# Four weight splits queued behind two transposed parts, and half of the merged sum transposed later

## The chip, the cores and the metric

The kernel runs on one core of one Trainium2 chip. The metric is device time of one execution in microseconds (us), lower is better; times are medians of repeated runs. The core's engines work side by side, each through its own queue in order: TensorE (PE; its weight loads are listed as PEld), VectorE (DVE), ScalarE (ACT), GpSimd (POOL), and SyncE (SP), which here only issues DMA transfers. An instruction starts when it is at the head of its queue and the semaphores it waits for have come.

## The reference

Two blocks in a row on 256 tokens of width 1024. The first normalises the tokens, projects them with `w_in`, runs dilated attention, a gated convolution and an attention to 256 memory rows, adds the three branches under gates, multiplies the sum with `w_out` onto the residual, and ends in a mixture of 32 experts, two per token. The second is a token mixer with scans and a feed-forward layer. What the change touches:

```python
kv  = rmsnorm(mem, g_mem) @ w_mem_kv      # memory: 256 x 1024 times 1024 x 1024
...
mg  = sum over branches of gate_b * (branch_b @ w_proj_b)   # 256 x 1024
x   = x + mg @ w_out                      # then the router, then the experts
```

## The kernel before, in words

**Products in two parts.** Every large product is made from operands cut in two: `hi`, a rounded copy, and `lo`, the remainder. `split` (L192) does this for 128 rows of a weight tile: ACT writes `hi` (L197), then POOL (L200) or DVE (L202), in turns, subtracts to give `lo`. `split_T` (L347) does it for activations that TensorE has transposed into PSUM: ACT writes the high part (L351), DVE the low part (L352) from the same PSUM bank. Two readers of one bank are kept apart, so the ACT copy of the next 128 columns waits for the DVE step of the ones before. `gemm_tm` (L227) then issues, for each of eight slices k and each of two token halves t, three products of 512 columns (L225): high part by `hi`, high part by `lo`, low part by `hi`. The split weights live in `hl`, five buffers for each part, so the splits run up to five slices ahead of the products.

**Generators.** After each slice `gemm_tm` calls `tick`, which advances work waiting in `self.side` by one `yield`.

**Order.** The code gives the order of the program. A planner of the framework (`schedule_with_timeline_sim`, L2102) then fixes each engine's queue by its own model of time: among the instructions that are ready in the model, it issues the one that stands earlier in the program. `issue_after(ins)` forces the instructions in its block behind `ins` on the same engine. The expert part up to its overflow test is planned in one piece with block 1.

**The start (L636 to L651).** The memory rows come in two halves of 512 columns, and the first two weight tiles of `w_mem_kv` (`w0`, four slices) beside them. `norm_T` (L365) transposes the memory (tile `pT`, four 128-column pieces in each of two tiles) and splits it into `hh` and `hl`; the scale is the gain `g_mem`, from `cols`. Then the product with `w_mem_kv`, columns 0 to 511 (keys), then 512 to 1023 (values).

**The merged sum (L717 to L762).** `mg` is held in two tiles, `mg[0]` for columns 0 to 511 and `mg[1]` for 512 to 1023. Its last contribution is added on DVE (`mt` L733, `mg` L735), for the second half right at the end of the last projection. L738 to L744 transpose both halves, four PSUM tiles `pmg` of two column pieces each, and split them into `mgh` and `mgl`. Then `eb.close()` gives back the space of `mg` and others, `open_first` opens five rings in it for early expert weights, and `w_out` is multiplied in two column halves, each over eight slices: slices 0 to 3 need `mg[0]`, slices 4 to 7 need `mg[1]`. The tag `acc` has four PSUM banks, shared by `pmg` and the two accumulators of each product. During the second column half the router's logits are begun (`first_half`).

Of the kernel before, what the change touches and what calls it, by code (L numbers as in the profile page):

```python
# [9 lines left out]
F32 = mybir.dt.float32  # L10
# [3 lines left out]
AF = mybir.ActivationFunctionType  # L14
# [35 lines left out]
def blocks(t):  # L50
    return [t[:, k, :] for k in range(t.shape[1])]


class Pools:


    def __init__(self, first, tags, second):
        self.of = lambda tag: first if tag in tags else second
# [5 lines left out]
class Builder:  # L64
# [21 lines left out]
    def __init__(self, tc, A, dbg):  # L86
        self.tc, self.nc, self.A, self.dbg = tc, tc.nc, A, dbg
        self.side, self.side2 = deque(), deque()
        self.started = False
        self.mem_first = self.lg = self.er = None  # L90
        self.first = []
        self.early = []
        self.mark = {}
        self.early_first = []
        self.ep = ExitStack()
        self.nt = 0
        self.pe = 0.0
        self.spent = 0.0
        self.es = ExitStack()
        self.nlo, self.lo, self.sp = 0, 2, 1024  # L100
# [77 lines left out]
    def wload(self, src, r0, n, c0, N, pairs=False):  # L178
# [10 lines left out]
        self.nc.sync.dma_start(out=t, in_=src[r0 * 128:(r0 + n) * 128, c0:c0 + N].rearrange("(k p) n -> p k n", p=128))  # L189
        return t  # L190

    def split(self, w, n, N):  # L192

        nc = self.nc
        hi = self.hl.tile([128, n, N], F32R, tag="hi", name="hi")
        lo = self.hl.tile([128, n, N], F32R, tag="lo", name="lo")
        nc.scalar.activation(out=hi, in_=w, func=AF.Copy)  # L197
        self.nlo += 1
        if self.nlo <= 0 or self.nlo % self.lo:
            nc.gpsimd.tensor_tensor(out=lo, in0=w, in1=hi, op=OP.subtract)  # L200
        else:
            nc.vector.tensor_tensor(out=lo, in0=w, in1=hi, op=OP.subtract)  # L202
        return hi, lo
# [143 lines left out]
    def split_T(self, ps, hi, lo, scale=None, imm=None):  # L347

        nc = self.nc
        s = scale if scale is not None else (1.0 if imm is None else imm)  # L350
        nc.scalar.activation(out=hi, in_=ps, func=AF.Copy, scale=s)  # L351
        nc.vector.scalar_tensor_tensor(out=lo, in0=ps, scalar=s, in1=hi, op0=OP.mult, op1=OP.subtract)  # L352

    def row_rstd(self, x):
# [10 lines left out]
    def norm_T(self, x, g, name, pool, normed=True):  # L365

        nc = self.nc
        hi = pool.tile([128, 8, 256], F32R, tag=name + "h", name=name + "h")
        lo = pool.tile([128, 8, 256], F32R, tag=name + "l", name=name + "l")
        xn = [x[:, t] for t in range(2)]  # L370
        if normed:
            r, xn = self.row_rstd(x)
            for t in range(2):
                nc.vector.tensor_scalar(out=xn[t], in0=x[:, t], scalar1=r[:, t:t + 1], scalar2=None, op0=OP.mult)
        for k in range(0, 8, 4):
            p = self.ps2.tile([128, 4, 256], F32, tag="ps2", name="pT")
            for j in range(4):
                for t in range(2):
                    nc.tensor.transpose(p[:, j, t * 128:(t + 1) * 128],
                                        xn[t][:, (k + j) * 128:(k + j + 1) * 128], self.ident)  # L380
            for j in range(4):
                self.split_T(p[:, j, :], hi[:, k + j, :], lo[:, k + j, :], scale=g[:, k + j:k + j + 1])
        return blocks(hi), blocks(lo)


# [218 lines left out]
    def block1(self):  # L604
        nc, A, tc = self.nc, self.A, self.tc
        es = ExitStack()
        ed = ExitStack()
        eb = ExitStack()
# [5 lines left out]
        def T(tag, name, shape, dt=F32, bufs=1):  # L614
            return (pa if tag in LATE else pb if tag in MID else self.pd).tile([128] + shape, dt, tag=tag, name=name, bufs=bufs)
# [30 lines left out]
        self.vm = T("a5", "vm", [2, 512])  # L646
        scaled = lambda dst: (lambda t, p: nc.scalar.activation(out=dst[:, t], in_=p, func=AF.Copy, scale=rm[0][:, t:t + 1]))
        self.early = w0
        self.gemm_tm(w_kv, 8, 0, 512, mT, scaled(self.km))
        self.load_x()  # L650
        self.gemm_tm(w_kv, 8, 512, 512, mT, scaled(self.vm))  # L651
# [65 lines left out]
        mg = [T(f"a{1 + i}", "mg", [2, 512]) for i in range(2)]  # L717
        for oi, (br, wn, nk) in enumerate([(2, "w_proj_mem", 4), (1, "w_proj_conv", 6), (0, "w_proj_attn", 2)]):
            bT = {0: (self.oah, self.oal), 1: (self.zh, self.zl), 2: (self.omh, self.oml)}[br]
            bT = [blocks(t) for t in bT]  # L720
            for half in range(2):
                G = T("G", "G", [2, 512], bufs=2)
                self.gemm_tm(w_in, 8, 5120 + br * 1024 + half * 512, 512, hT, lambda t, p: nc.scalar.activation(
                    out=G[:, t], in_=p, func=AF.Tanh, scale=0.5), tick=2)
# [10 lines left out]
                        nc.vector.tensor_tensor(out=d, in0=d, in1=m, op=OP.add)  # L735
                self.gemm_tm(A[wn][0], nk, half * 512, 512, bT, ev)
        mgh, mgl = T("hh", "mgh", [8, 256], F32R), T("hl", "mgl", [8, 256], F32R)
        for b in range(0, 8, 2):  # L738
            p = self.acc.tile([128, 2, 256], F32, tag="acc", name="pmg")
            for j in range(2):  # L740
                for t in range(2):
                    o = 128 * ((b + j) % 4)
                    nc.tensor.transpose(p[:, j, 128 * t:128 * t + 128], mg[b // 4][:, t, o:o + 128], self.ident)
            self.split_T(p, mgh[:, b:b + 2], mgl[:, b:b + 2], imm=0.5)  # L744
        lg = self.logits(self.acc, "acc", [T(f"a{6 + i}", "x1T", [4, 256]) for i in range(2)], lambda: T("mt", "junk", [512], bufs=2))

        def first_half():
            yield
            yield
            next(lg)  # L750

        self.drain()
        self.finish2()
        eb.close()
        self.open_first(self.nearly)
        for half in range(2):
            hs = slice(half * 512, half * 512 + 512)
            self.gemm_tm(A["w_out"][0], 8, half * 512, 512, (blocks(mgh), blocks(mgl)), lambda t, p: nc.vector.tensor_tensor(
                out=self.x[:, t, hs], in0=p, in1=self.x[:, t, hs], op=OP.add), late=self.late0 * half)
            if half == 0:  # L760
                self.side.append(first_half())
        self.drain()  # L762
        deque(lg, maxlen=0)
# [1342 lines left out]
```

## Time and profile before

| | us |
|---|---|
| median of 3 runs (lowest to highest) | 1489.14 (1488.11 to 1493.19) |
| profiled execution | 1496.53 |
| its span, first to last instruction | 1494.8 |
| PE busy in the span | 1374.6 |
| DVE / ACT / POOL busy | 839.4 / 632.1 / 571.4 |
| mean granted TensorE clock | 0.968 |

Matmuls overlap, so a duration listed for one is longer than its share of the time; the distance from one start to the next is the measure. A row of the timeline gives start, duration, engine, line, operation, output<-inputs and a count; rows of equal neighbours are merged. The square bracket is idle time of the engine before the row and what ended it. In the rows `hh`, `hl` are the parts of the transposed memory, `mgh`, `mgl` those of the merged sum.

### The profile page before, as it was taken

The numbers are of one execution on the slowest core, as the hardware profiler recorded it, in microseconds if no ns is written. First come the engines' busy times: TensorE is split into PE (matmuls) and PEld (weight loads), VectorE is DVE, ScalarE is ACT, GpSimd is POOL, SyncE is SP. The second block draws the span as 40 slices with busy tenths as digits, with TensorE's granted clock in tenths as the row PEclk, the third lists the DMA queues.
The fourth block names the chain that finished last, engine by engine and source line by source line (L and its number), as shares of the span: only waits on it lengthen the run. The fifth ranks groups of instructions, "written<-read, shape, count | busy, mean of one in ns | idle before, by whom it ended". The sixth has DMA issues, their size and how long they took to land. (4 is left out here: it accounts for less than half of the span.)

```text
span 1494.8 us, 25833 instructions
## 1 busy us (share of the span) xinstructions
PE 1374.6 (92%) x10187; PEld 1091.2 (73%) x10188; DVE 839.4 (56%) x1570; ACT 632.1 (42%) x1308; POOL 571.4 (38%) x438
## 2 busy tenths in 40 slices
PE   7999999999988898998898979998989799799997
PEld 6778877876655664765565649896889687699985
DVE  6684574444324646533465537888669965833334
ACT  6675434543313213120322225556747434455543
POOL 3433225441100012130002214478965634567764
PEclk9999999999999999999999999999999999899998
DMA  8758659976999999999989882521334214455551
GB/s 290 243 180 307 250 222 346 354 265 221 401 389 409 406 397 405 396 414 379 394 355 412 314 309 93 170 87 55 113 100 127 85 58 141 135 191 183 172 203 49
DMA packets 135307, 374.37 MB, mean 250 GB/s; under 512 B 12472, under 2 KB 26639, under 8 KB 123919
## 3 DMA queue, kind: packets, MB, share of 16 engines
q1 hardware_dynamic: 135183, 372.69, 67.6%
q8 instruction: 81, 1.33, 0.4%
q14 instruction: 43, 0.35, 0.1%
HBM read 371.61 MB, written 1.06 MB: 249 GB/s over the span
## 5 line engine op out<-in xcount | busy, mean ns | idle before, releaser
L200 POOL TENSOR_TENSOR lo<-w,hi 128x512 fp32r<-128x512 f32 x262 | 363.0, 1392 | 377.1 <-ACT hi L197 329.2
L197 ACT ACTIVATE hi<-w 128x512 fp32r<-128x512 f32 x436 | 270.2, 630 | 264.6 <-PE acc L225 243.5
L202 DVE TENSOR_TENSOR lo<-w,hi 128x512 fp32r<-128x512 f32 x174 | 156.5, 900 | 204.9 <-ACT hi L197 204.4
L225 PE MATMUL acc<-xh,lo 128*128 128x256 f32 x576 | 165.3, 289 | 3.4 <-DVE lo L202 3.4
L225 PE MATMUL acc<-xl,hi 128*128 128x256 f32 x576 | 166.6, 290 | 0.0
L225 PE MATMUL acc<-xh,hi 128*128 128x256 f32 x576 | 166.1, 290 | 0.0
L796 PE MATMUL gu<-w,xg 128*32 128x256 f32 x2048 | 132.6, 383 | 0.0
L225 PEld LDWEIGHTS acc<-xh,lo 128*128 128x128 f32 x576 | 112.5, 196 | 4.0 <-DVE lo L202 3.6
L225 PEld LDWEIGHTS acc<-xl,hi 128*128 128x128 f32 x576 | 112.9, 196 | 0.5 <-issue 0.2
L225 PEld LDWEIGHTS acc<-xh,hi 128*128 128x128 f32 x576 | 113.1, 197 | 0.2
L796 PEld LDWEIGHTS gu<-w,xg 128*32 128x32 f32 x2048 | 65.8, 110 | 50.9 <-issue 8.9
L225 PE MATMUL acc<-cT,w 128*128 128x256 f32 x416 | 99.2, 391 | 2.1 <-DMA w<-in_w_in_dram 2.1
L1423 POOL TENSOR_TENSOR U<-U,Z 128x512 f32<-128x512 f32 x32 | 41.4, 1296 | 150.0 <-DVE Z L1422 148.1
L225 PEld LDWEIGHTS acc<-cT,w 128*128 128x128 f32 x416 | 79.1, 195 | 22.3 <-issue 8.9
L1411 POOL TENSOR_TENSOR U<-U,Z 128x512 f32<-128x512 f32 x8 | 13.8, 1729 | 197.6 <-ACT y L827 99.0
L225 PE MATMUL acc<-lo,hh 128*128 128x512 f32 (+1 forms) x224 | 87.8, 394 | 0.0
L225 PE MATMUL acc<-hi,hl 128*128 128x512 f32 (+1 forms) x224 | 86.0, 393 | 1.2 <-DVE hl L352 1.2
L225 PE MATMUL acc<-hi,hh 128*128 128x512 f32 (+1 forms) x224 | 81.6, 398 | 5.5 <-ACT hh L351 5.5
L1304 DVE SCALAR_TENSOR_TENSOR cva<-acc,cwg,cva 128x248 f32<-128x248 f32 (+3 forms) x160 | 72.0, 473 | 19.7 <-ACT cva L1298 18.0
L825 DVE COPY y<-yq 32x256 f32<-32x256 f32 x64 | 27.0, 422 | 89.7 <-ACT y L827 89.3
L820 PE MATMUL yq<-w,hT 128*32 128x256 f32 x1024 | 71.3, 419 | 5.0 <-ACT hT L814 5.0
L1403 ACT ACTIVATE V<-U 128x512 f32<-128x512 f32 x40 | 25.7, 642 | 97.4 <-POOL U L1423 80.6
(539 smaller groups left out, 2908.2 us busy)
## 6 DMA issues: line engine op xcount, KB each, us to landing
w<-in_w_in_dram SPq DMA_DIRECT2D x71, 1024.0 KB
w<-in_w_gate_dram SPq DMA_DIRECT2D x64, 1024.0 KB
w<-in_w_up_dram SPq DMA_DIRECT2D x64, 1024.0 KB
w<-in_w_down_dram SPq DMA_DIRECT2D x64, 1024.0 KB
w<-in_w_ada_dram SPq DMA_DIRECT2D x24, 1024.0 KB
w<-in_w_out_dram SPq DMA_DIRECT2D x12, 1024.0 KB
w<-in_w_ffn_gate_dram SPq DMA_DIRECT2D x11, 1024.0 KB
w<-in_w_ffn_up_dram SPq DMA_DIRECT2D x11, 1024.0 KB
```

Of the source, the lines that this page charges most:

```text
L197: nc.scalar.activation(out=hi, in_=w, func=AF.Copy)
L200: nc.gpsimd.tensor_tensor(out=lo, in0=w, in1=hi, op=OP.subtract)
L202: nc.vector.tensor_tensor(out=lo, in0=w, in1=hi, op=OP.subtract)
L225: return self.nc.tensor.matmul(out, lhsT=lhsT, rhs=rhs, start=start, stop=stop, skip_group_check=True)
L796: last = nc.tensor.matmul(gu[32 * j:32 * j + 32, :], lhsT=xg[:, k, s0:s0 + 32], rhs=w[k // 4][:, k % 4, 256 * (j % 2):256 * (j % 2) + 256] ...
L820: nc.tensor.matmul(yq[32 * q:32 * q + 32, :], lhsT=hT[:, b, 32 * half:32 * half + 32], rhs=wd[kb // 2][:, kb % 2, 256 * q:256 * q + 256], ...
L825: nc.vector.tensor_copy(o, i)
L1304: nc.vector.scalar_tensor_tensor(out=av[:, :, d], in0=pv[:, :, s], scalar=wc(k), in1=av[:, :, d], op0=OP.mult, op1=OP.add)
L1403: nc.scalar.activation(out=cut(bt["V"], b), in_=view(bt["U"], b), func=AF.Copy)
L1411: nc.gpsimd.tensor_tensor(out=view(U, b), in0=view(U, b), in1=cut(Z, b), op=OP.add)
L1423: nc.gpsimd.tensor_tensor(out=view(U, b), in0=view(U, b), in1=cut(Z, b), op=OP.add)
```

## The change

`held` puts the next four ACT copies of `split` behind the instruction stored in `self.hold`. That is the second `split_T` of the memory (its columns 128 to 255), and the four copies are those of the first four weight slices. The transposes and splits of `mg[1]` become `merged(1)`, called from `self.side` at the third tick of the first `w_out` half, that is after its third slice in program order. `eb.close()` and `open_first` move behind the first half of `w_out`, since `mg[1]` is still needed.

```diff
+    def held(self):
+        n, after = self.hold
+        self.hold = n - 1, after
+        return self.tc.issue_after(after.ins) if n > 0 else ExitStack()
...
-        nc.scalar.activation(out=hi, in_=w, func=AF.Copy)
+        with self.held():
+            nc.scalar.activation(out=hi, in_=w, func=AF.Copy)
...
-        nc.scalar.activation(out=hi, in_=ps, func=AF.Copy, scale=s)
+        self.mark["parts"] = nc.scalar.activation(out=hi, in_=ps, func=AF.Copy, scale=s)
...
+                if k + j == 1:
+                    self.first_parts = self.mark["parts"]
...
+        self.hold = 4, self.first_parts
         self.gemm_tm(w_kv, 8, 0, 512, mT, scaled(self.km))
...
-        for b in range(0, 8, 2):
-            p = self.acc.tile([128, 2, 256], F32, tag="acc", name="pmg")
+        def merged(half):
+            for b in (4 * half, 4 * half + 2):
+                p = self.acc.tile([128, 2, 256], F32, tag="acc", name="pmg")
...
+        def merged_late():
+            yield
+            yield
+            merged(1)
+
+        merged(0)
...
-        eb.close()
-        self.open_first(self.nearly)
+        self.side.append(merged_late())
         for half in range(2):
...
             if half == 0:
+                eb.close()
+                self.open_first(self.nearly)
                 self.side.append(first_half())
```

## Rows read from the trace of the kernel before

**Rows 1.** The page's first part: busy us, share, instructions.
```profile
PE 1374.6 (92%) x10187; PEld 1091.2 (73%) x10188; DVE 839.4 (56%) x1570; ACT 632.1 (42%) x1308; POOL 571.4 (38%) x438
```
**Rows 2.** Windows: stretch, length, busy per engine, PEclk, DMA share, GB/s.
```profile
50.00:323.00 273.00, 273.00 (x1584) 215.64 (x1582) 159.83 (x280) 141.74 (x263) 105.51 (x75) 1.00 0.75 270
323.03:329.49 6.46, 4.55 (x17) 3.51 (x17) 3.49 (x6) 0.84 (x3) 1.14 (x1) 0.74 0.90 319
327.00:328.00 1.00, 1.00 (x4) 0.81 (x3) 0.00 (x0) 0.00 (x0) 0.00 (x0) 0.50 0.92 348
360.00:370.00 10.00, 9.38 (x112) 6.56 (x114) 6.62 (x39) 1.70 (x3) 0.00 (x0) 1.00 0.19 71
```
**Rows 3.** Timeline, all engines, around the merged sum's transposes.
```profile
321.99 1.04 PE L743 MATMUL pmg<-cst,mg 128*128 128x128 f32 x8
322.38 1.27 DVE L733 SCALAR_TENSOR_TENSOR mt<-G,acc 128x512 f32<-128x512 f32 x2
322.73 1.07 ACT L351 ACTIVATE mgh<-pmg 128x512 fp32r<-128x512 f32 x2
322.90 1.27 POOL L200 TENSOR_TENSOR lo<-w,hi 128x512 fp32r<-128x512 f32 x1 [0.99 <-ACT hi L197]
323.57 1.15 DVE L735 TENSOR_TENSOR mg<-mg,mt 128x512 f32<-128x512 f32 x1
324.64 0.68 DVE L352 SCALAR_TENSOR_TENSOR mgl<-pmg,mgh 128x512 fp32r<-128x512 f32 x1
324.78 0.44 PE L743 MATMUL pmg<-cst,mg 128*128 128x128 f32 x2 [1.75 <-DVE mg L735]
325.38 0.50 PE L225 MATMUL acc<-hi,mgh 128*128 128x512 f32 x1 [0.16 <-DVE mgl L352]
326.41 0.63 PE L225 MATMUL acc<-hi,mgh 128*128 128x512 f32 x1
326.83 0.63 PE L225 MATMUL acc<-lo,mgh 128*128 128x512 f32 x1
328.54 1.19 PE L743 MATMUL pmg<-cst,mg 128*128 128x128 f32 x6
329.49 0.48 PE L225 MATMUL acc<-hi,mgh 128*128 128x512 f32 x1
```
**Rows 4.** Timeline, all engines, the first product with the memory's weights.
```profile
7.74 0.19 DVE L343 COPY cols<-pcol 128x34 f32<-128x34 f32 x1 [1.88 <-PE pcol L342]
8.88 1.15 ACT L197 ACTIVATE hi<-w 128x512 fp32r<-128x512 f32 x2 [6.63 <-DMA w<-in_w_mem_kv_dram]
9.94 0.46 ACT L351 ACTIVATE hh<-pT,cols 128x256 fp32r<-128x256 f32 x1
10.45 1.22 PE L225 MATMUL acc<-hi,hh 128*128 128x512 f32 x2 [2.74 <-ACT hh L351]
11.33 0.47 DVE L352 SCALAR_TENSOR_TENSOR hl<-pT,cols,hh 128x256 fp32r<-128x256 f32 x1
11.84 0.47 ACT L351 ACTIVATE hh<-pT,cols 128x256 fp32r<-128x256 f32 x1 [0.41 <-DVE hl L352]
12.21 1.05 ACT L360 ACTIVATE xn<-mem 128x1024 f32<-128x1024 f32 x1
13.17 1.91 PE L379 MATMUL pT<-cst,mem 128*128 128x128 f32 x8
15.53 0.40 PE L225 MATMUL acc<-hi,hh 128*128 128x512 f32 x1
15.76 0.39 PE L225 MATMUL acc<-lo,hh 128*128 128x512 f32 x1
18.18 0.50 PE L225 MATMUL acc<-hi,hh 128*128 128x512 f32 x1 [0.20 <-ACT hh L351]
19.64 0.74 PE L225 MATMUL acc<-hi,hl 128*128 128x512 f32 x2 [0.27 <-DVE hl L352]
```
**Rows 5.** Waits of PE from 360 to 880 us: total, times, longest.
```profile
PE tph L812 <- DVE hh L809: 22.8, 19, 1.8
```

More of the change, by code (lines that the diff above doesn't have):

```diff
@@ L97, in __init__ @@
         self.pe = 0.0
+        self.hold = 0, None
         self.spent = 0.0
@@ L737, in block1 @@
         mgh, mgl = T("hh", "mgh", [8, 256], F32R), T("hl", "mgl", [8, 256], F32R)
-        for b in range(0, 8, 2):
-            p = self.acc.tile([128, 2, 256], F32, tag="acc", name="pmg")
[L740 to L744, printed above, removed]
+        def merged(half):
+            for b in (4 * half, 4 * half + 2):
+                p = self.acc.tile([128, 2, 256], F32, tag="acc", name="pmg")
+                for j in range(2):
+                    for t in range(2):
+                        o = 128 * ((b + j) % 4)
+                        nc.tensor.transpose(p[:, j, 128 * t:128 * t + 128], mg[half][:, t, o:o + 128], self.ident)
+                self.split_T(p, mgh[:, b:b + 2], mgl[:, b:b + 2], imm=0.5)
+        def merged_late():
[3 more added lines that the diff above has]
+        merged(0)
         lg = self.logits(self.acc, "acc", [T(f"a{6 + i}", "x1T", [4, 256]) for i in range(2)], lambda: T("mt", "junk", [512], bufs=2))
```

## The prediction

> **What bounds the kernel now.** I read the busy shares first, then the windows, then the timeline at the two places that the change touches. PE is busy 92% of the span [rows 1]. The windows say that before the experts this is close to a hard bound: PE is busy for all of the 273 us from 50 to 323 at a granted clock of 1.00 [rows 2]. So a gap of PE removed there moves everything after it, unless a later wait takes it back. At the merged sum there is such a gap: 6.46 us in which PE is busy 4.55, at a mean clock of 0.74, with 0.50 for the whole microsecond from 327 [rows 2]. 0.50 is 1.2 GHz, 1.00 is 2.4 GHz. The expert stretch from 366 to 860 us has PE busy 445.83 of 494.00 us and DMA at a share of 0.97 [rows 2]. Both restart from the first expert: between 360 and 370 us the DMA share is 0.19, as the rings are full and wait for PE to use weights. An earlier PE therefore starts the transfers earlier too, and I pass the gain through this stretch in full.
>
> **The second edit, at 323 us.** Before, eight transposes of `mg[0]` start at 321.99 and are over at 323.03. PE's next instruction is a transpose of `mg[1]`, which waits for DVE's last addition and starts at 324.78: an idle of 1.75 us. The first product comes at 325.38, since its accumulator takes the PSUM bank of the first `pmg`, which DVE's `mgl` has to release [rows 3]. The clock then falls: products start 0.42 us apart at 326.41 and 326.83, where 0.23 is the distance at full clock (15.53 to 15.76) [rows 3, 4]. Six more transposes follow at 328.54, and from 329.49 on the products run in a row. So 6.46 us hold eight products and eight transposes. At full clock these are 8 x 0.23 + 8 x 0.13 (1.04 over eight) = 2.9 us. At most 3.6 us can be won: about 1.9 of idle, the rest the half clock.
>
> After the change the first three slices of `w_out` (18 products) stand ahead of the `mg[1]` transposes. The two accumulators are now allocated right after two `pmg` and not four, so by the turn of the four banks they take those of the last projection, free when `mt` ends at 323.65 (322.38 + 1.27), the first half of that pair at about 323.0. The first product then waits for `mgh` alone: half of the pair that starts at 322.73, so 323.3 [rows 3]. The weights of these slices were split ahead; the last subtraction, on POOL, ends at 324.17. Until the low part exists PE has eight products that need only the high part (two slices, two token halves, `hi` and `lo`): 1.8 us, to 325.2. The low part ends at 325.32 (324.64 + 0.68) [rows 3]. New idle: 0.3 before the first product and 0.2 before the low part, 0.5 in all. Two waits of 0.20 and 0.27, 1.5 us apart, stand at 18.18 and 19.64 [rows 4], and the clock did not fall after them, so I keep it at full. The term is 3.6 - 0.5 = 3.1 us.
>
> What moves with it: eight transposes, two ACT copies, two DVE parts. They are late next: the transposes start after 18 products, 323.3 + 0.2 + 4.1 = 327.6, and end near 328.6; the first low part is there 0.5 + 0.6 + 0.7 us after the start (four transposes, half of 1.07, 0.68), at 329.4. Slice 3's six products run until 330.0 and cover it. If that cover failed, the price is up to 0.7 us. `eb.close()` is later in the program, but the five rings it gives wait for the `mg[1]` transposes either way (329.5 before), and SP's queue of weight loads behind them has the 8 us of DMA idle between 360 and 370 as cover. If the second half's accumulators had to wait for the first half's release, it would cost two additions of about 0.7 us and another half-clock stretch; I take 0, since two banks are free by then. Bounds of this term: 0.3 (PE's order puts low-part products early, see the first rival) to 3.6.
>
> The Trainium skill, page "SBUF — State Buffer", section "Who interferes with whom", says that a DVE instruction with two SBUF inputs and a GpSimd instruction that reads SBUF exclude each other for the whole instruction. The trace agrees: the addition to `mg[1]` at 323.57 takes 1.15 us and ends 0.55 after POOL's subtraction, while the next addition-sized step, 324.64, takes 0.68 with POOL idle [rows 3]. It speaks against the change a little: DVE cannot be early with the low part while POOL splits `w_out`, so the wait of 0.2 stays. If the two only shared, the term would be 3.3 and not 3.1.
>
> **The first edit, at 8 us.** ACT idles until the first weight tile lands at 8.88, copies two weight slices, and only then the first transposed part (`hh`, 9.94), though its gain was ready at 7.93 (7.74 + 0.19). The first product starts at 10.45, on that part [rows 4]. Behind the change ACT does `hh` at 7.95 to 8.4, DVE the low part to 8.9 (0.47), ACT the second `hh` to 9.4 (the same bank, so it must wait, as at 11.84), and the first weight copy from 9.4 to 9.95, where it ended about 9.5 before. First product 10.0 instead of 10.45: 0.45 won. ACT has then done two parts in time that was idle, and loses the 0.41 us wait at 11.84. Later PE waits of 0.20 at 18.18 and 0.27 at 19.64 are on ACT's and DVE's parts [rows 4] and can shrink. I take 0.8 us. Queued behind the held copies are POOL's and DVE's subtractions, each 0.45 us later for the first slice, covered by the low-part products that can now come first.
>
> Bounds: above, PE without a stall. 24 products end at 20.1 before (19.64 + 2 x 0.23). From 10.0, six at 0.43 make 12.6; eight transposes at that clock, 1.6, 14.2; two more at 0.43, 15.0; 16 at 0.23 end at 18.7: a gain of 1.4. Below: the planner may put the two squares of 1.05 (12.21) ahead of the held copies, 2.1 us less the 0.45, a loss of 1.6. I go by the nearest rows, the waits that are named. From 20 us on PE is in a row, so the gain lasts.
>
> **Sum.** 3.1 + 0.8 = 3.9 us of the profiled 1496.53, giving 1492.6. The median is 7.4 us below that execution; I take the same 3.9 off: 1485.2.
>
> **The rivals.** *The wait only changes its name.* The planner thinks the low part is there sooner and puts its products third, in the program's order, as they stood at 325.38 and after. PE then does two products, idles from 323.8 to 325.4, and the clock falls as before. The second term shrinks to the two products, 0.5; with some 0.5 from the start, 1488.1. For it: the program's order, and the 1.15 us addition that a model without the exclusion puts at 0.67. Against: the model must also see the low part behind two additions. *Slower: the expert loop.* The experts are planned in the same piece, so a shift of some us changes which side work stands beside which expert. There PE waited for DVE before the transpose of the hidden values 19 times, 22.8 us, 1.2 each [rows 5]. It decides from the fourth further wait, which eats the gain; seven more, 8.4 us, give 1493.6. For it: the trace has 13 of 32 experts without such a wait, so there is room. Against: both sides shift together. *The loop goes the other way.* Four waits fewer: 1480.4. *The first edit does nothing*, since ACT is busy later all the same: 1486.0, inside the forecast's own range.
>
> **How the numbers follow.** The forecast has 0.57, the wait renamed 0.18, slower 0.14, the loop better 0.11. What a measurement can tell here is about 0.3%, 4.5 us: faster is below 1484.7, slower above 1493.6. The forecast's own range, 1483.3 (3.6 + 1.4, and some of the runs' spread) to 1488, lies across the first edge, with about 0.4 of it below: 0.23. With the better loop 0.10 and a little of the rest, faster is 0.35. Slower is half of its case and 0.03 from the loss at the start: 0.10. Same is 0.55. The 80% range is 1480.5 to 1492.5: it leaves out the far half of the slower case and most of the better loop.
>
> **What would show it.** At the merged sum: the first `mgh` product within 0.5 us of the eighth transpose, no idle of 1 us before the low part, a clock of 1.00 through 325 to 330, and eight transposes behind 18 products. At the start: `hh` on ACT before 8.5, the first product near 10.0, the same place in the keys' product 0.5 to 1.4 us earlier. At the first expert's product a lead of about 3.9 us over the kernel before, unchanged at 860. It is wrong if PE idles again before `mgl` or slice 4, if the lead at the first expert is under 2, or if it is lost between 366 and 860.

## The result, and the profile after

| | before | after |
|---|---|---|
| median of 6 runs (lowest to highest), us | 1489.41 (1488.10 to 1493.19) | 1512.19 (1507.78 to 1519.67) |
| ratio, 95% interval | | 1.0142 (1.0118 to 1.0166) |
| span of the profiled execution, us | 1494.8 | 1516.5 |
| mean granted TensorE clock in it | 0.968 | 0.959 |

The changed kernel is slower by 21 us by the ratio (the two medians lie 22.8 us apart). In the changed kernel L225 is L233, L351 is L359, L743 is L755, and L812 is L833.

Where the 21.7 us between the two profiled spans arise is read from three moments: PE's first transpose `tph` of the first expert, the one of the last expert, and PE's last product. "Half clock" is the time that the trace lists at a granted clock of 0.50, summed over the stretch.

| stretch, us | before | after | difference |
|---|---|---|---|
| start to first expert (half clock) | 373.4 (13.7) | 369.2 (3.4) | -4.2 |
| first to last expert (half clock) | 507.5 (34.1) | 520.1 (47.8) | +12.6 |
| last expert to the end (half clock) | 602.5 (41.0) | 615.8 (64.9) | +13.3 |

So a lead of 4 us, as forecast, is there at the first expert in these two profiles (2.5 us of it by luck, as shown below), and 26 us are lost behind it, where the change has no line. The page's first line, then PE's wait that my slower rival named, from 360 to 890 us [rows 1, 5]:

```profile
PE 1389.4 (92%) x10187; PEld 1102.6 (73%) x10188; DVE 839.0 (55%) x1570; ACT 632.6 (42%) x1308; POOL 568.1 (37%) x438
```
```profile
PE tph L833 <- DVE hh L830: 24.1, 19, 2.1
```

PE does the same 10187 products and is busy 15 us longer. It waits for `hh` as often as before, 19 times, for 24.1 us instead of 22.8.

At the two edited places the timeline shows the moves that I described. At the start ScalarE does `hh` ahead of the weights [rows 4]; at the merged sum the first product stands 0.33 us behind the eighth transpose, and the other eight transposes follow among the products [rows 3]:

```profile
7.87 0.47 ACT L359 ACTIVATE hh<-pT,cols 128x256 fp32r<-128x256 f32 x1 [5.61 <-DVE cols L351]
9.27 2.18 ACT L205 ACTIVATE hi<-w 128x512 fp32r<-128x512 f32 x4
9.94 1.22 PE L233 MATMUL acc<-hi,hh 128*128 128x512 f32 x2 [2.34 <-ACT hi L205]
...
320.11 1.03 PE L755 MATMUL pmg<-cst,mg 128*128 128x128 f32 x8
321.48 0.50 PE L233 MATMUL acc<-hi,mgh 128*128 128x512 f32 x1 [0.33 <-ACT mgh L359]
323.51 0.73 PE L233 MATMUL acc<-hi,mgl 128*128 128x512 f32 x2 [0.84 <-DVE mgl L360]
326.37 0.60 PE L755 MATMUL pmg<-cst,mg 128*128 128x128 f32 x4
327.27 0.60 PE L755 MATMUL pmg<-cst,mg 128*128 128x128 f32 x4
```

What else differs is the order of the queues. The planner gave 1324 of PE's 7352 places to other instructions than before. In the traces none of them lies between 65 us and the merged sum or in the feed-forward layer. Beside the two edited places (the first reaches to 65 us) they lie between the experts and in the second block's mixer.

### The profile page after: what moved, and what is told of

The parts are those of the page before. It is cut to its first block, busy times and chain, and to the rows that moved or that the text cites. A ratio compares the mean times of both kernels' runs of the same rounds, so it can differ in the third digit from the quotient of the medians.

```text
span 1516.5 us, 25834 instructions
## 1 busy us (share of the span) xinstructions
PE 1389.4 (92%) x10187; PEld 1102.6 (73%) x10188; DVE 839.0 (55%) x1570; ACT 632.6 (42%) x1308; POOL 568.1 (37%) x438
## 5 line engine op out<-in xcount | busy, mean ns | idle before, releaser
L210 DVE TENSOR_TENSOR lo<-w,hi 128x512 fp32r<-128x512 f32 x174 | 152.3, 877 | 202.3 <-ACT hi L205 199.6
L233 PE MATMUL acc<-xh,lo 128*128 128x256 f32 x576 | 166.1, 290 | 3.4 <-DVE lo L210 3.4
L233 PE MATMUL acc<-xl,hi 128*128 128x256 f32 x576 | 167.4, 291 | 0.0
L233 PE MATMUL acc<-xh,hi 128*128 128x256 f32 x576 | 166.5, 290 | 0.0
L817 PE MATMUL gu<-w,xg 128*32 128x256 f32 x2048 | 136.4, 387 | 0.0
L233 PEld LDWEIGHTS acc<-xh,lo 128*128 128x128 f32 x576 | 112.8, 197 | 4.4 <-DVE lo L210 3.6
L233 PEld LDWEIGHTS acc<-xl,hi 128*128 128x128 f32 x576 | 113.3, 197 | 0.8 <-issue 0.7
L233 PEld LDWEIGHTS acc<-xh,hi 128*128 128x128 f32 x576 | 113.3, 197 | 0.6 <-issue 0.5
L233 PE MATMUL acc<-cT,w 128*128 128x256 f32 x416 | 99.6, 393 | 1.9 <-DMA w<-in_w_in_dram 1.9
L233 PEld LDWEIGHTS acc<-cT,w 128*128 128x128 f32 x416 | 79.8, 197 | 21.7 <-issue 8.4
L233 PE MATMUL acc<-hi,hl 128*128 128x512 f32 (+1 forms) x224 | 85.8, 390 | 3.5 <-DVE hl L360 3.5
L233 PE MATMUL acc<-lo,hh 128*128 128x512 f32 (+1 forms) x224 | 87.8, 395 | 0.0
L233 PE MATMUL acc<-hi,hh 128*128 128x512 f32 (+1 forms) x224 | 81.1, 397 | 2.5 <-ACT hi L205 2.3
L233 PE MATMUL X<-T,W 128*128 128x128 f32 x384 | 57.2, 296 | 17.0 <-issue 6.4
```

Of the source, the lines that this page charges most:

```text
L233: return self.nc.tensor.matmul(out, lhsT=lhsT, rhs=rhs, start=start, stop=stop, skip_group_check=True)
L817: last = nc.tensor.matmul(gu[32 * j:32 * j + 32, :], lhsT=xg[:, k, s0:s0 + 32], rhs=w[k // 4][:, k % 4, 256 * (j % 2):256 * (j % 2) + 256] ...
```

## The experiments

The kernels were timed in four groups, each beside the kernel before, and a ratio is always within a group. The median of the kernel before was 1494.0 us in the first group, then 1491.9, 1491.9 and 1493.2. The three dots mark lines left out of a code cut; the comments behind `#` are added here.

**Either edit alone, and the order written out (four kernels).** To hold an order, each engine's queue of one kernel was read out, and in the other kernel each instruction was queued behind its predecessor in that list:

```diff
+def pin(tc, block):
+    here = {i.name: i for i in tc.nc.cur_bb.bb.instructions}
+    for engine in ("PE", "Activation", "DVE", "Pool", "SP"):
...
+            tc.add_manual_dep(here[name], last, mybir.DependencyInfo(
+                mybir.DependencyClass.NoSync, mybir.DependencyReason.DATA), reason="issue_after")
+            last = name
```

The first edit alone, as lines added to the kernel before:

```diff
+        with self.held():
+            nc.scalar.activation(out=hi, in_=w, func=AF.Copy)
...
+                if k + j == 1:
+                    self.first_parts = self.mark["parts"]
...
+        self.hold = 4, self.first_parts
         self.gemm_tm(w_kv, 8, 0, 512, mT, scaled(self.km))
```

> Only the first edit (four held copies at the start); the merged sum as before. Theory A, the order: the loss of the changed kernel lies in the planner's new order of the side work between the experts and in the second block, not in either edit's own place. In this kernel 396 of TensorE's 7352 places are taken otherwise than before, against 1324 in the changed kernel, and the second block has nearly the order of before. So a lead of 1 to 2 us at the merged sum, a part of the 12.6 us lost between the experts (order there differs, but less), little of the 12.4 us lost after them: 1488 to 1500. Rival B, the timing: whatever runs earlier meets transfers and clock falls elsewhere; a lead of 1.9 us would cost about 1.9/4.4 of the loss, some 11 us: about 1500, with the loss spread over both stretches. Rival C, the five weight rings that open later in the program: not in this kernel, so 1488.

Measured: 0.9996 (0.9975 to 1.0017).

The second edit alone, as the changed kernel with nothing held:

```diff
-        self.hold = 4, self.first_parts
+        self.hold = 0, self.first_parts
```

> Only the second edit (second half of the merged sum transposed between the two halves of w_out, rings opened there); no copy is held at the start. Theory A, the order: the loop's order is the one of the kernel with the first edit alone (none of TensorE's places from the experts on until two thirds of the queue differ between these two), the second block nearly that of before; so about the same time as that kernel, within 4 us: 1486 to 1500, and the lead of 2.5 us at the logits is seen. Rival B, the timing: a lead of 2.5 us, some 14 us lost: about 1503. Rival C, the later rings: the whole loss, 1508 to 1514.

Measured: 0.9983 (0.9964 to 1.0003). Neither edit alone costs anything beyond its interval, though each makes the planner order the loop anew, in part. Rival C is out: the rings open late here too. So is B, which wanted 11 to 14 us.

Both edits, with the order of before behind them:

```diff
+        pin(tc, 1)          # the queues of the kernel before
         with tc.If(n > 0):
...
         build(tc, A, {})
+        pin(tc, 2)          # and of its second block
```

> Both edits, and from the work traced after the merged sum's end on, every engine's queue is written out in the order that the kernel before has (one weight load of w_in is queued behind the branch after the experts and not ahead of it). Theory A, the order: the lead of about 4.4 us at the first expert stays to the end: 1485, 1483 to 1487.5, and the half-clock time from 890 us on is that of before. Rival B, the timing: the lead is lost between the experts and in the second block as in the changed kernel: 1505 to 1514. Rival C, the later rings: 1500 or more, lost between the experts.

Measured: 1.0004 (0.9983 to 1.0025). The whole loss is gone. So is the gain of 4 us that I expected to be left.

Neither edit, with the order of the changed kernel behind the merged sum:

```diff
+        pin(tc, 1)          # the queues of the changed kernel
         with tc.If(n > 0):
...
         build(tc, A, {})
+        pin(tc, 2)
```

> Neither edit: the kernel before, with every engine's queue from the work after the merged sum on written out in the order that the changed kernel has. Theory A, the order: no lead and the whole loss: 1489.4 + 25 = 1514, 1508 to 1520. Rival B, the timing, and rival C, the rings: 1489, as before, since nothing runs earlier and the rings open where they did.

Measured: 1.0139 (1.0096 to 1.0181). The order alone makes the loss: the kernel before, with not one instruction added or taken away, is as slow as the changed one.

**Which part of the order.** The order of the changed kernel in one stretch, that of before in the other; neither edit:

```diff
+        pin(tc, 1)          # in the first kernel the changed queues, in the second those of before
...
+        pin(tc, 2)          # the other way round
```

> Neither edit; the queues are the kernel before's, but for the stretch from the merged sum to the end of the experts, which is written out in the order of the changed kernel (610 of TensorE's places). The order of both stretches cost 19 us (1.0139). By the traces of that run and of the one with both edits in the old order, about 6 us of it were lost by the last expert and 13 behind it. Theory A, each stretch's order costs by itself: 6 us, 1500, 1497 to 1503. Rival D, the experts' order alone causes both, as it leaves the second block in another state of clock and transfers: 1510 or more. Rival E, only the second block's order counts and the loss between the experts is taken up by transfers: 1494.

Measured: 1.0095 (1.0074 to 1.0117), 14 us.

> Neither edit; the queues are the kernel before's up to the end of the experts, and from the second block on they are written out in the order of the changed kernel (579 of TensorE's places). Theory A: 13 us, 1507, 1503 to 1510, with stretches of 13.7 and 17.1 us at half clock near 895 and 1110 as in both kernels that have this order, where the others have 3.4. Rival D, the experts' order causes all: 1494 and no such stretches. Rival E, all of it lies here: 1513.

Measured: 1.0054 (1.0033 to 1.0074), 8 us. The two add up to 22 us, so each stretch costs by itself, but my split was wrong: the larger part is between the experts. I had counted a half-clock stretch at 895 us to the second block's order. The kernel with the experts' order alone has one there too (17.1 us at 904), and so has the kernel with the second edit in the order of before, below (17.1 us at 879), while the kernel with the second block's order alone has only 3.4 us at a time there: that one is no sure mark of either order. The one near 1105 is there as expected, though 10.2 us long and not 17.1.

**Each edit with the order of before.** As the two kernels with one edit each, with

```diff
+        pin(tc, 1)          # the queues of the kernel before
...
+        pin(tc, 2)
```

> The second edit alone, with the order of before written out for everything behind it. Between the experts' start and the end this is the kernel before. The second edit's own gain was 2.3 to 2.9 us in traces where the kernel beside it had half-clock time at the merged sum, and 0.1 to 0.5 against one that had none there. Theory A: 0.1 to 2.9 us faster than before, 0.9981 to 1.0000 of it. Rival: the first edit was worth its 2 us after all, and this kernel is no better than the one with both edits: 1.0004.

Measured: 1.0000 (0.9978 to 1.0021). The interval holds both answers.

> The first edit alone, with the order of before written out for everything behind it. In the profile before, the first weight tile reached ScalarE's queue at 8.88 us; in two later executions without the held copies at 7.28 and 7.11, and there the first product came at 8.84 and 8.68, against 9.63 to 9.94 with the held copies. Theory F, the first edit was sized against an execution with a late tile: it costs 1 to 2 us, ratio 1.0007 to 1.0014, and the eight transposes of the merged sum start near 320.5 where kernels without it have them near 318.5. Rival, my forecast of 0.8 us gained: 0.9995 and transposes 0.8 us earlier than in the kernels of this call without the edit.

Measured: 0.9995 (0.9978 to 1.0012), with the transposes at 320.2 us. This decides neither way at the end.

**A shift without the change.** The first eight transposes of the merged sum are repeated:

```diff
-            for j in range(2):
+            for _ in range(4 if b < 4 else 1):      # 16 and not 4 in the third kernel
+                for j in range(2):
...
+        pin(tc, 1)          # in the second and third: the queues of before
```

> Neither edit. The first eight transposes of the merged sum are done four times over (24 more, same result), 24 x 0.13 = 3.1 us of work; the order of all else is left to the planner. It then orders the second block on VectorE, ScalarE and GpSimd exactly as in the changed kernel, and the stretch between the experts nearly so (VectorE: 28 places of 1610 differ), although here the work behind comes later and not earlier. Theory A, the order: 3.1 + 19 to 22 us, 1511 to 1517, ratio 1.013 to 1.017. Rival B, the loss comes from the edits (an earlier start, late rings): 3.1 us, 1495, ratio 1.002. Rival G, an order written out costs something by being written out: also 1.002, as nothing is written out here.

Measured: 1.0095 (1.0060 to 1.0129), 14 us: less than expected, but far from 3. Rivals B and G are out, since neither edit is made here and no order is written out.

> As the kernel with 24 more transposes, with the order of before written out behind them. The same work, the same delay, only the order differs. Theory A: 3.1 us slower than before, 1495, ratio 1.000 to 1.004. Rival B: the same as its sister with the planner's order.

Measured: 0.9980 (0.9950 to 1.0009). The same work in the old order costs nothing: 1.75 of the 3.1 us lie in PE's idle before the `mg[1]` transposes [rows 3], and from the first `pmg` transpose to the first expert the two profiles take 50.7 and 50.3 us, no more than the 49.8 to 51.7 of eight kernels without the added work. So some added work, which is no part of the change and hardly delays the chip, sends the planner to nearly the same costly order.

> The first eight transposes of the merged sum done sixteen times over (120 more, 120 x 0.13 = 15.6 us), with the order of before written out behind them. It asks whether a shift at the merged sum reaches the end, as my sum had it. Full passage: 15.6 us, ratio 1.0105, 1.008 to 1.013, and the first expert as much later as the last. Theory H, the stretch between the experts is set by transfers that start by themselves, so that a shift is taken up there: under 6 us, ratio below 1.004.

Measured: 1.0085 (1.0051 to 1.0119), 13 us. From the merged sum to the first expert this kernel takes 12.1 us longer than the mean of eight without additions (63.0 against 50.9). It arrives in full as far as the interval can tell; theory H falls.

**What a worse order costs by.** Products of constants are put into PE's longest waits for `hh`:

```diff
+        if e in FILL:
+            with self.tc.issue_after(last.ins):
+                for _ in range(FILL[e]):
+                    fill = self.mm(tp, self.bits[:, 0], self.bits.rearrange("p i n -> p (i n)")[:, None].to_broadcast([128, 2, 256]), True, True)
...
+FILL = {e: 5 for e in (4, 6, 7, 8, 14, 15, 20, 21, 23, 24, 30)}   # 12 experts in the order of the changed kernel
```

> Neither edit, the order of before written out. In 11 of the 32 experts (those with an idle of 1.56 to 1.76 us before the transposes of the hidden values) five products of constants are added behind the last gate product, 5 x 0.24 = 1.2 us each; their result is overwritten by the transposes. In the profiles nearly every fall of the clock between the experts stands behind such an idle. Theory K, the clock: most of the 21 to 41 us at half clock between the experts goes, and half of it is won: first to last expert 490 to 496 us instead of 501 to 509, the kernel 1476 to 1484, ratio 0.990 to 0.995. Rival L, the stretch is set by transfers, so that TensorE's clock is no loss there: 1492, 1.000. Rival M, the added products delay what stands behind them: up to 11 x 1.2 = 13 us slower, 1.003 to 1.009.

Measured: 0.9986 (0.9970 to 1.0002). Between the experts the time at half clock is 20.5 us, and the stretch 504.8. No theory comes out as written: K is wrong by size, M by sign, and L fits by the time alone, though the scatter of the stretch with the clock, in the table below, speaks against it. I had said that nearly every fall of the clock stands behind such an idle. In the seven unfilled profiles with this order it is 34 of 63 falls between the experts (I counted a fall to an idle if it begins within 6 us of its end); the others stand behind none of the filled waits.

> As the kernel with the changed order between the experts alone (14 us slower than before), with five products of constants in each of the 12 experts where that order has an idle of 1.3 to 2.1 us before the transposes. Theory N, the order costs 6 us by itself and the rest by the clock: first to last expert 496 to 500 us, 5 to 7 us more than in the kernel with the order of before and filled waits; the kernel 8 to 12 us faster than without the added products, 1495 to 1499, ratio 1.002 to 1.005. Rival K only, all of the cost is the clock: both filled kernels agree within 3 us. Rival L, the clock costs nothing between the experts: 1507, 1.0095 as without the products.

Measured: 1.0021 (1.0003 to 1.0039), by the two ratios 11 us less than the same order without the products; stretch 510.3 us, half clock 20.5. It stands 6.0 us (4.7 to 7.3, from the single runs) behind its sister, the kernel before this one. That difference and the gain are as theory N has them; the stretch is not (496 to 500 expected).

> The second edit alone, the order of before written out, and the five products in each of the 11 experts. Theory K: as the kernel with the filled waits alone or up to 2 us faster (no half clock at the merged sum): 1474 to 1484, ratio 0.988 to 0.995. Rival: the second edit gives nothing at the end, as without the filled waits (1.0000): the same time as its sister.

Measured: 0.9959 (0.9941 to 0.9976), 1487.55 us against 1493.16: the one version that beats both kernels. It is 3.2 us (1.8 to 4.7) faster than its sister without the second edit.

## Why the prediction was wrong

**The step that failed** is "I pass the gain through this stretch in full". It took the order between the experts as given and moved it as a whole. A shift does pass in full when the order is held (the 120 transposes: 12.1 us at the first expert, 13 at the end). But the order was not held: the planner places each piece of the second block's work by its modelled moment, and a few us at the merged sum change which piece stands beside which expert. I had written this premise down under the slower rival, with a chance of 0.14, and put it aside with "both sides shift together". The price that I gave it was wrong too: no wait for `hh` was added, 19 before and 19 after. And the rival named only the expert loop: the new order of the second block's mixer behind it, 8 us of the 21, stands nowhere in the prediction. The stretch was read from this row of the trace before (columns as in [rows 2]):

```profile
366.00:860.00 494.00, 445.83 (x4350) 300.75 (x4349) 230.75 (x471) 124.40 (x302) 62.35 (x53) 0.97 0.97 386
```

It shows how busy the engines are in one order, and not what another order costs.

**What the order costs by, between the experts.** The same stretch in the profiles (T is first to last expert):

| order between the experts | profiles | T, us | half clock, us | T less half of it |
|---|---|---|---|---|
| of before | 7 | 501.2 to 509.4 | 20.5 to 41.0 | 488.9 to 491.1 |
| of either edit alone | 2 | 506.8, 507.3 | 34.1, 34.1 | 489.8, 490.2 |
| of the changed kernel | 3 | 515.6 to 521.7 | 37.5 to 47.8 | 496.2 to 497.8 |
| of the 24 transposes, left to the planner | 1 | 515.8 | 41.0 | 495.3 |
| of before, waits filled | 2 | 504.8, 505.4 | 20.5, 20.5 | 494.6, 495.1 |
| of the changed kernel, waits filled | 1 | 510.3 | 20.5 | 500.1 |

T scatters by 8 us within one order, and half of the half-clock time accounts for nearly all of that. (The Trainium skill, page "TensorE: Matmul & The Clock Gate", section "Terms", puts the penalty at the throttled time times one minus the clock's ratio, which is this half; the last column's scatter of 2 us agrees.) From the first row to the third T rises by 12.5 us on the mean: 6.6 in the last column and 5.9 by 11.7 us more at half clock. The filled kernels have equal half-clock time and still differ by 5 us: that part is not the clock (a twelfth filled expert, by the 4.6 us below for eleven, would be some 0.4 of it).

How the work moves is seen at two turns, from the `tph` of the 12th expert to that of the 14th, and then over the whole stretch (columns as in [rows 2]). The kernel with the first edit and the order of before:

```profile
529.16:566.07 36.91, 34.82 (x332) 24.92 (x332) 25.07 (x50) 10.89 (x25) 6.23 (x6) 1.00 1.02 406
370.01:874.23 504.22, 454.02 (x4433) 305.77 (x4431) 234.69 (x481) 127.58 (x309) 62.39 (x53) 0.97 0.98 391
```

The kernel without an edit in the order of the changed one, the same experts:

```profile
529.50:572.81 43.31, 37.57 (x333) 25.71 (x333) 25.42 (x50) 10.22 (x24) 6.70 (x6) 0.96 0.99 389
368.68:884.28 515.60, 461.84 (x4433) 307.36 (x4431) 237.56 (x481) 127.14 (x309) 62.05 (x53) 0.96 0.97 382
```

The two turns hold the same products (one more or less is at the edge of the window), but 20 of them have moved from the 12th turn to the 13th, and the two take 43.3 us instead of 36.9. PE is idle for 5.7 us of them instead of 2.1: it waits 1.7 and 2.1 us for `hh` where the old order has one wait of 0.5. Other turns become shorter, so this is one place and not the sum.

Over the whole stretch, on the means of the first and third rows, the 6.6 us of the last column are 3.5 us more idle time of PE (53.9 instead of 50.4) and 3.1 us more in which it is listed as busy with the same products, half of the half-clock time taken off. Weights that come late are an obvious suspect, as the DMA engines are busy for 0.98 and 0.97 of the two stretches, but PE is not seen to wait for them longer. The wait that a load of `w_in` ends is nearly all there is (with the rest 0.5 to 2.1 us in the seven profiles of the first row and 1.9 to 2.2 in the three of the third), here in these two kernels:

```profile
PE acc L233 <- DMA w<-in_w_in_dram: 1.2, 2, 0.7
PE acc L225 <- DMA w<-in_w_in_dram: 2.2, 1, 2.2
```

Nor does the side work come in larger lumps: the products in one expert's turn go from 70 to 230 in the old order and from 70 to 226 in the new. What makes these 6 us over the whole stretch stays open; the runs show that the order makes them, and that the clock alone does not.

**In the second block it is nearly all the clock.** From the last expert to the end, half of the half-clock time taken off, all 16 profiles give 579.5 to 583.3 us, whatever the order. The half-clock time is 34 to 51 us in ten profiles with the old order there (mean 41.0), and 44.4 to 64.9 in the four with the new one (mean 54.7): half of the difference is 6.8 us, of the 8 measured. Between 1100 and 1140 us those four list 10.2 to 17.1 us at half clock in one piece, all others 3.4. The place is seen by one window, 1095 to 1115 us, in the kernel with the new order in the second block alone:

```profile
1095.00:1115.00 20.00, 18.05 (x100) 16.86 (x100) 15.00 (x40) 9.19 (x21) 8.02 (x7) 0.67 0.26 80
```

and in the kernel with the first edit and the old order, first all, then the instructions on `acc` alone:

```profile
1095.00:1115.00 20.00, 16.73 (x130) 16.41 (x129) 14.40 (x39) 9.73 (x20) 5.18 (x4) 0.91 0.29 99
```
```profile
1095.00:1115.00 20.00, 7.25 (x47) 6.39 (x46) 6.09 (x15) 2.13 (x5) 0.91 0.29 99
```

The kernel with the new order, on `acc` alone:

```profile
1095.00:1115.00 20.00, 0.00 (x0) 0.00 (x0) 5.70 (x14) 2.12 (x5) 0.67 0.26 80
```

The old order puts 47 products of the input projection between the short products of the scans. The new one has none there: PE works through the scans' chain by itself, at a mean clock of 0.67, and is listed as busy longer. That the clock falls for want of these products is my reading; no run put products there.

**The second edit, forecast at 3.1 us.** The moves were right; the size depends on the clock. From the first `pmg` transpose to the first expert the profiles with the edit take 49.1 to 49.5 us (five). Without it, and without added transposes, they take 49.8 (three, no half clock at the merged sum) or 51.4 to 51.7 (five, with it): a gain of 0.6 or 2.3, and 1.6 on the mean of the eight. The profile that I worked from was one of the five. The wait for `mgl` was 0.84 and not 0.2, since the planner put four products, and not eight, ahead of the low part. (For an addition with POOL idle I had taken the 0.68 us of `mgl`, which reads PSUM and is another instruction; the second addition to `mg` in that trace, at 325.25, took 0.67, so that reading stands.) At the end the two pairs of kernels give 0.0 (within 3 us) and 3.2 us; which is nearer stays open.

**The first edit, forecast at 0.8 us.** I sized it against one execution, in which the first weight tile came at 8.88 us and the first product at 10.45 [rows 4]. In eleven other profiles without the edit the tile comes between 7.11 and 8.17, the first product at 8.68 to 9.73; with it, at 9.63 to 9.94 (four). One of the eleven, ScalarE and PE:

```profile
7.11 1.15 ACT L197 ACTIVATE hi<-w 128x512 fp32r<-128x512 f32 x2 [4.86 <-DMA w<-in_w_mem_kv_dram]
```
```profile
8.68 1.22 PE L225 MATMUL acc<-hi,hh 128*128 128x512 f32 x2 [1.32 <-ACT hh L351]
```

With the edit the first product is thus 0.5 us later on the mean (9.77 against 9.26), and the `pmg` transposes 1.0 us later (320.5 against 319.5, single ones 318.1 to 320.9). So the term is about -1 at the merged sum by these means, at the end (0.9995) not told from 0, and not +0.8. Of the 4.2 us lead at the first expert, 2.5 are the late start of the profile before, whose `pmg` transposes stand at 322.0: that the lead agreed with the forecast was luck.

The sum was thus 3.9 forecast, about 1 in place, and the order took 21.

## What to carry to other kernels

Where a planner orders a long stretch by its model of time, a local edit is two changes: its own, and a new order of all that is planned with it. Hold the order behind the edit fixed to measure the first; and price the second from what other orders of the same kernel cost (here from no measurable difference to +21 us), not from the edit. A step is to be sized on several profiles: both of my local terms came from one execution, late at one place and at half clock at the other.

## What was not expected of the hardware

The granted clock can fall to half behind a short idle of PE. In the kernel with the first edit and the old order PE waits 1.70 us for `hh`, and the clock is 0.51 from 411.41 on:

```profile
409.63 0.31 PE L823 MATMUL tph<-cst,hh 64*128 64x64 f32 x2 [1.70 <-DVE hh L820]
410.31 2.68 PE L831 MATMUL yq<-w,hT 128*32 128x256 f32 x32 [0.37 <-ACT hT L825]
```
```profile
404.60:411.41 6.81, 4.75 (x86) 2.61 (x82) 2.09 (x4) 0.66 (x2) 0.00 (x0) 1.00 0.94 366
411.41:414.82 3.41, 3.41 (x36) 1.74 (x32) 0.84 (x2) 0.75 (x2) 0.00 (x0) 0.51 1.01 400
```

Not every such idle is followed by a fall: between the experts of this kernel 7 of 14 idles of more than 1.5 us are, and 9 of 15 in the kernel before (counted as above). With five products in the wait of the same expert, 0.42 us of it are left and the clock stays:

```profile
411.85 1.25 PE L225 MATMUL tph<-bits 128*128 128x512 bf16 x5
413.53 0.34 PE L817 MATMUL tph<-cst,hh 64*128 64x64 f32 x2 [0.42 <-DVE hh L815]
```
```profile
406.80:417.00 10.20, 9.41 (x137) 5.64 (x139) 3.14 (x6) 1.03 (x3) 0.00 (x0) 1.00 0.83 317
```

The products are not free: with them T less half of the half-clock time is 4.6 us longer (494.8 against 490.3), which took back most of the clock's gain of 6 us (20.5 us at half clock instead of 32.7).
